# Column roll by 100 on one core: head loads of 1280 B between 256 B boundaries, in place of 1024 B that begin 112 B past one

## The chip, the cores and the metric

The kernel runs on one core of one Trainium2 chip. The metric is device time in microseconds (us). Timed alone, the kernel before took 817.23 us, the median of three runs (817.18 to 818.21). Every other time here is from one profiled execution of it.

## The reference

The kernel shifts each row of an 8192 x 8192 float32 matrix by 100 columns, cyclically:

```python
def reference(x, shift):            # x: 8192 x 8192 float32, shift = 100
    return np.roll(x, shift, axis=1)
```

So out[r, 100:] is x[r, :8092], and out[r, :100] is x[r, 8092:]. Nothing is calculated: 268 MB are read and 268 MB are written.

## The kernel before, in words

The kernel cuts each output row at column a = 256. With s = 100 (the shift), the head of a row is its first 256 columns, of which the first s come from the end of the same input row and the other g = a - s = 156 from its beginning. The bulk is the rest, columns 256 to 8191.

**The bulk** (lines 36 to 43) never enters the core's own memory. Two hardware queues, SP's and ACT's, issue 264 copies each from DRAM to DRAM. Most of them have 16 rows of 7936 floats (31,744 B a row, 496 KB a copy); in the last four blocks each is cut into two halves of 248 KB. All of it goes out from one line, L43, in the order of the loop, j = 0 and 2 from SP and j = 1 and 3 from ACT.

**The heads** (lines 60 to 80) go through SBUF, the core's own memory, and all their DMAs are issued by POOL (GpSimd). A stage k takes 512 rows: 128 partitions with Q = 4 neighbouring rows each; there are 16 stages. The last 100 columns of row r and the first 156 of row r + 1 are neighbours in DRAM, so one run of 256 floats (1024 B) that straddles the row boundary brings the wrapped part of one row and the beginning of the next. A stage does this:

- L72 loads t, [128, 3, 256]: for each partition the three straddling runs between its four rows. 128 x 3 = 384 runs of 1024 B, 384 KB.
- L73 loads the last 100 columns of the fourth row straight into h, 400 B a partition.
- L74 (DVE) copies the wrapped parts of rows 0 to 2 from t to h, 300 floats a partition.
- L76 loads the first 156 columns of row 0 straight into h, 624 B a partition.
- L77 (DVE) copies the beginnings of rows 1 to 3 from t to h, 468 floats a partition.

After the 16 stages of loads, L80 issues 16 stores of h (512 KB each, rows of 1024 B) into the output. Both pools have 16 buffers, so no tile waits for another to come free. POOL's instructions stand in the program's order: all loads, then all stores. From the ninth POOL DMA on, each waits for an earlier one's semaphore, of which there are eight.

The line that the change is about is the address of the straddling run (L70 and L71):

```python
lead = bass.AP(tensor=x.tensor, offset=(k * P * Q + 1) * n_cols - s,
               ap=[[Q * n_cols, P], [n_cols, Q - 1], [1, a]])
```

A row of x has 32,768 B, a multiple of 256. A run begins 400 B ahead of a row's beginning, which is 112 B past a 256 B boundary, and ends 624 B behind it, which is 144 B short of one.

Of the kernel before, what the change touches and what calls it, by code (L numbers as in the profile page):

```python
# [1 line left out]

# [4 lines left out]


@with_exitstack
def kernel(  # L10
    ctx: ExitStack,
    tc: tile.TileContext,
    x: bass.AP,
    shift: int,
    out: bass.AP,
):
    nc = tc.nc
    n_rows, n_cols = x.shape
    s = shift % n_cols
    a = -(-s // 128) * 128  # L20
    if 0 < a <= 384 and a + 128 <= n_cols:
        a += 128
    g = a - s
    P = nc.NUM_PARTITIONS
    engines = [nc.sync, nc.scalar]
    n_chunks = 16
    rows = n_rows // n_chunks

    xm = x.rearrange("(c e j) w -> c j e w", e=16, j=4)
    om = out.rearrange("(c e j) w -> c j e w", e=16, j=4)
    if a < n_cols:
        blocks = n_rows // 64
        mid = (a + n_cols) // 256 * 128
        for c in range(blocks):
            parts = ((a, mid), (mid, n_cols)) if c >= blocks - 4 and a < mid else ((a, n_cols),)  # L40
            for j in range(4):
                for lo, hi in parts:
                    engines[j % 2].dma_start(out=om[c, j, :, lo:hi], in_=xm[c, j, :, lo - s:hi - s])  # L43
    if a == 0:
        return


    if a > 512:
        for i in range(n_chunks):
            r = slice(i * rows, (i + 1) * rows)  # L50
            nc.gpsimd.dma_start(out=out[r, :s], in_=x[r, n_cols - s:])
            if g > 0:
                nc.gpsimd.dma_start(out=out[r, s:a], in_=x[r, :g])
        return

    Q = 4  # L60
    n_st = n_rows // (P * Q)
    reads = ctx.enter_context(tc.tile_pool(name="reads", bufs=n_st))
    heads = ctx.enter_context(tc.tile_pool(name="heads", bufs=n_st))
    xt = x.rearrange("(k p q) c -> k p q c", q=Q, p=P)
    ot = out.rearrange("(k p q) c -> k p q c", q=Q, p=P)
    tiles = []
    for k in range(n_st):
        t = reads.tile([P, Q - 1, a], x.dtype)
        h = heads.tile([P, Q, a], x.dtype)
        lead = bass.AP(tensor=x.tensor, offset=(k * P * Q + 1) * n_cols - s,  # L70
                       ap=[[Q * n_cols, P], [n_cols, Q - 1], [1, a]])  # L71
        nc.gpsimd.dma_start(out=t[:], in_=lead, single_packet=True)  # L72
        nc.gpsimd.dma_start(out=h[:, Q - 1, :s], in_=xt[k, :, Q - 1, n_cols - s:], single_packet=True)  # L73
        nc.vector.tensor_copy(h[:, :Q - 1, :s], t[:, :, :s])  # L74
        if g > 0:
            nc.gpsimd.dma_start(out=h[:, 0, s:], in_=xt[k, :, 0, :g], single_packet=True)  # L76
            nc.vector.tensor_copy(h[:, 1:, s:], t[:, :, s:])  # L77
        tiles.append(h)
    for k, h in enumerate(tiles):
        nc.gpsimd.dma_start(out=ot[k, :, :, :a], in_=h[:], single_packet=True)  # L80


# [1 line left out]
_INS = ['x', 'shift']  # L84
_OUTS = [((8192, 8192), 'float32')]

_NUMBERS = {'shift': 100}


# [26 lines left out]
```

## Time and profile before

| what | value |
|---|---|
| median of three timed runs | 817.23 us (817.18 to 818.21) |
| profiled execution, span from first to last instruction | 813.9 us |
| what the timed median has beyond that span | 3.3 us |
| DVE busy | 12.0 us, 1% of the span, 32 copies |
| POOL busy | 41.1 us, 5% of the span, 68 instructions |
| bulk copies: moved by queues q1 and q10 | 260.08 MB |
| heads: moved by queue q0 | 16.78 MB (8.39 loaded, 8.39 stored) |
| straddling load t<-in_x_dram | 16 of 384 KB, 48.9 us from issue to landing (median) |
| head store out_dram<-h | 16 of 512 KB, 102.9 us from issue to landing (median) |
| bulk copy of 496 KB | 12.5 us from issue to landing (median) |

The span is the time of the profiled execution; its page gives no time beyond the span, so what lies around it is taken from the timed median. In the profile's page, q1 and q10 are the two hardware queues (bulk), q0 is POOL's software queue (heads). The share of a DMA queue is the time that its packets took, over the 16 DMA engines' time. A packet that waits for its data counts as taking time, so a share near 100% does not say that an engine moves bytes at its own limit. A DRAM-to-DRAM byte is counted once in MB and GB/s, but is read from DRAM once and written to it once; a byte of a head load or store touches DRAM once only.

### The profile page before, as it was taken

How to read it: one execution, taken by the hardware profiler on the slowest of the kernel's cores; microseconds unless marked ns; L12 is line 12 of the kernel's file. 1: busy time of each engine (PE TensorE's matmuls, PEld its weight loads, DVE VectorE, ACT ScalarE, POOL GpSimd, SP SyncE). 2: the span in 40 equal slices, each digit the busy share in tenths (PEclk: the TensorE clock that was granted, in tenths of full speed). 3: DMA queues.
4: the chain of work that ended last, by engine and by line, in shares of the span. 5: the costliest groups of instructions: out<-in, count | busy, mean ns of one | idle time of the engine just before them, and what ended most of it. 6: DMA issues, size and time to landing. Idle time of an engine off the chain costs nothing. (4 is left out here: it accounts for less than half of the span.)

```text
span 813.9 us, 689 instructions
## 1 busy us (share of the span) xinstructions
DVE 12.0 (1%) x32; POOL 41.1 (5%) x68
## 2 busy tenths in 40 slices
DVE  0000000000000000000000000000000000000000
POOL 2000011111000100000000000000000000000000
DMA  9999999999999999999999999999999999999998
GB/s 314 346 340 344 353 346 350 344 351 344 346 355 346 345 362 354 353 357 354 355 355 349 342 335 331 335 332 325 335 328 332 334 337 334 332 337 332 334 314 293
DMA packets 22277, 276.90 MB, mean 340 GB/s; under 512 B 9472, under 2 KB 9728, under 8 KB 13824
## 3 DMA queue, kind: packets, MB, share of 16 engines
q1 hardware_dynamic: 8448, 130.04, 45.9%
q10 hardware_dynamic: 8448, 130.04, 44.3%
q0 software_dynamic: 5376, 16.78, 8.9%
q14 instruction: 5, 0.04, 0.0%
HBM read 268.44 MB, written 268.44 MB: 660 GB/s over the span
## 5 line engine op out<-in xcount | busy, mean ns | idle before, releaser
L80 POOL DMA_DIRECT2D out_dram<-h x16 | 11.4, 713 | 139.5 <-DMA out_dram<-h 92.5
L76 POOL DMA_DIRECT2D h<-in_x_dram x16 | 8.6, 540 | 158.4 <-DMA t<-in_x_dram 158.4
L72 POOL DMA_DIRECT2D t<-in_x_dram x16 | 12.2, 760 | 32.1 <-DMA h<-in_x_dram 31.3
L73 POOL DMA_DIRECT2D h<-in_x_dram x16 | 8.9, 558 | 32.7 <-DMA h<-in_x_dram 32.7
L74 DVE COPY h<-t 128x300 f32<-128x300 f32 x16 | 5.9, 367 | 268.4 <-DMA t<-in_x_dram 268.4
L77 DVE COPY h<-t 128x468 f32<-128x468 f32 x16 | 7.5, 468 | 0.0
L97 POOL MEMSET const-float32-0.0<- 128x1 f32 x1 | 0.1, 98 | 0.2 <-issue 0.2
L97 POOL MEMSET const-bfloat16-1.0<- 128x1 bf16 x1 | 0.1, 101 | 0.0
L97 POOL MEMSET const-float32-1.0<- 128x1 f32 x1 | 0.1, 98 | 0.0
L97 POOL MEMSET const-uint8-127<- 128x1 uint8 x1 | 0.1, 98 | 0.0
## 6 DMA issues: line engine op xcount, KB each, us to landing
out_dram<-in_x_dram ACTq DMA_DIRECT2D x248, 496.0 KB, 12.5
out_dram<-in_x_dram SPq DMA_DIRECT2D x248, 496.0 KB, 12.5
out_dram<-h POOLq DMA_DIRECT2D x16, 512.0 KB, 102.9
t<-in_x_dram POOLq DMA_DIRECT2D x16, 384.0 KB, 48.9
out_dram<-in_x_dram SPq DMA_DIRECT2D x16, 248.0 KB, 5.9
out_dram<-in_x_dram ACTq DMA_DIRECT2D x16, 248.0 KB, 5.9
h<-in_x_dram POOLq DMA_DIRECT2D x16, 78.0 KB, 41.9
h<-in_x_dram POOLq DMA_DIRECT2D x16, 50.0 KB, 47.2
```

Of the source, the lines that this page charges most:

```text
L72: nc.gpsimd.dma_start(out=t[:], in_=lead, single_packet=True)
L73: nc.gpsimd.dma_start(out=h[:, Q - 1, :s], in_=xt[k, :, Q - 1, n_cols - s:], single_packet=True)
L74: nc.vector.tensor_copy(h[:, :Q - 1, :s], t[:, :, :s])
L76: nc.gpsimd.dma_start(out=h[:, 0, s:], in_=xt[k, :, 0, :g], single_packet=True)
L77: nc.vector.tensor_copy(h[:, 1:, s:], t[:, :, s:])
L80: nc.gpsimd.dma_start(out=ot[k, :, :, :a], in_=h[:], single_packet=True)
L97: nc = _bacc.Bacc("TRN2", target_bir_lowering=False, num_devices=1)
```

## The change

The straddling run is widened at both ends to the next multiple of 64 floats (256 B): lo = 128 floats ahead of the row's beginning (100 are used) and hi = 192 floats behind it (156 are used). A run has 320 floats, 1280 B, and begins and ends on a 256 B boundary. The tile t grows to [128, 3, 320], 480 KB a stage. The two DVE copies take the same 300 and 468 floats out of the middle of the runs. All other loads, the stores and the bulk are as they were, and so is the order of the instructions on every engine.

```diff
     Q = 4
+    lo, hi = -(-s // 64) * 64, -(-g // 64) * 64
...
-        t = reads.tile([P, Q - 1, a], x.dtype)
+        t = reads.tile([P, Q - 1, lo + hi], x.dtype)
         h = heads.tile([P, Q, a], x.dtype)
-        lead = bass.AP(tensor=x.tensor, offset=(k * P * Q + 1) * n_cols - s,
-                       ap=[[Q * n_cols, P], [n_cols, Q - 1], [1, a]])
+        lead = bass.AP(tensor=x.tensor, offset=(k * P * Q + 1) * n_cols - lo,
+                       ap=[[Q * n_cols, P], [n_cols, Q - 1], [1, lo + hi]])
         nc.gpsimd.dma_start(out=t[:], in_=lead, single_packet=True)
         nc.gpsimd.dma_start(out=h[:, Q - 1, :s], in_=xt[k, :, Q - 1, n_cols - s:], single_packet=True)
-        nc.vector.tensor_copy(h[:, :Q - 1, :s], t[:, :, :s])
+        nc.vector.tensor_copy(h[:, :Q - 1, :s], t[:, :, lo - s:lo])
         if g > 0:
             nc.gpsimd.dma_start(out=h[:, 0, s:], in_=xt[k, :, 0, :g], single_packet=True)
-            nc.vector.tensor_copy(h[:, 1:, s:], t[:, :, s:])
+            nc.vector.tensor_copy(h[:, 1:, s:], t[:, :, lo:lo + g])
```

## The prediction

> **What bounds the kernel now.** I read the engines' row first, then the DMA rows of the page, then who SP waits for, then the DMA queues stage by stage.
>
> ```profile
> DVE 12.0 (1%) x32; POOL 41.1 (5%) x68
> ...
> DMA  9999999999999999999999999999999999999998
> ...
> q1 hardware_dynamic: 8448, 130.04, 45.9%
> q10 hardware_dynamic: 8448, 130.04, 44.3%
> q0 software_dynamic: 5376, 16.78, 8.9%
> ...
> HBM read 268.44 MB, written 268.44 MB: 660 GB/s over the span
> ```
>
> No engine computes for long; the DMA engines are never free. The chain of waits is of no use here: it follows POOL and stops at 403 us, while bulk copies are issued until 807 us. SP's own waits name what ends last:
>
> ```profile
> SPq L43 <- DMA out_dram<-in_x_dram: 667.0, 260, 4.5
> ```
>
> For 667 of 814 us SP waits for earlier bulk copies to land. So the kernel ends when the bulk ends, and the heads cost only what they take away from it. What do the two share? Three windows tell: 20 to 280 us (head loads beside the bulk), 290 to 410 us (head stores beside it), 520 to 780 us (bulk alone). Columns: packets, MB, share of the 16 DMA engines.
>
> ```profile
> q1 hardware_dynamic: 2572, 40.83, 41.9%
> q10 hardware_dynamic: 2568, 40.70, 39.5%
> q0 software_dynamic: 3136, 8.69, 18.4%
> ```
>
> ```profile
> q1 hardware_dynamic: 1183, 18.79, 46.5%
> q10 hardware_dynamic: 1182, 18.76, 42.3%
> q0 software_dynamic: 1406, 5.11, 12.2%
> ```
>
> ```profile
> q10 hardware_dynamic: 2726, 43.24, 49.9%
> q1 hardware_dynamic: 2728, 43.30, 49.6%
> ```
>
> Count a bulk byte twice (read and written in DRAM) and a head byte once. Loads: (2 x 81.53 + 8.69) MB / 260 us = 660.6 GB/s. Stores: (2 x 37.55 + 5.11) / 120 = 668.4. Bulk alone: 2 x 86.54 / 260 = 665.7. Counted simply, the rates are 347, 356 and 333 GB/s and differ by 7%; as DRAM traffic they agree within 1.2%. **The bound is DRAM traffic, about 660 to 668 GB/s in every stage**, whoever asks for it. All traffic over the rate of bulk alone, (2 x 260.08 + 16.78) MB / 665.7 GB/s, gives 806.6 us of the 813.9; 2.0 us more is the lower rate beside the loads (5.1 GB/s x 260 us = 1.33 MB), and the other 5.3 us lie in the start, the tail and the edges of my windows.
>
> **The change part by part.**
>
> *More bytes read.* 16 loads x 384 runs x 256 B = 1.573 MB more from DRAM (t goes from 6.29 to 7.86 MB). They are asked for in the load stage, so they cost 1.573 MB / 660.6 GB/s = **2.4 us**, by which the bulk, and with it the end, moves back. This is the one term on the path.
>
> Whether 256 B more that is asked for is 256 B more that DRAM delivers, the trace of before does not show. Ends: at the low end the shortfall of the load stage (1.33 MB, 2.0 us) is all waste at the ends of the misaligned runs, fetched already and thrown away, and the change costs 2.4 - 2.0 = +0.4 us; zero is possible within the scatter of that shortfall. At the high end DMA engine time is what is short: q0 took 18.4% of 260 us = 47.8 us for 8.69 MB beside the loads, 5.51 us per MB, so 1.573 MB would take 8.7 us (at the stores' price, 12.2% of 120 us for 5.11 MB = 2.86 us per MB, 4.5 us). I take 2.4 us, since the three stages agree in DRAM traffic and in no other count, and keep the ends.
>
> The load stage being the one that is below the others speaks for some waste there. The Trainium skill (DMA: Bandwidth & Descriptors, "How a descriptor splits into AXI transactions") says that a read which starts off a 256 B boundary begins its first transaction at the boundary below, and that the bytes ahead of its start still cost 32 B beats. By it I estimate 8 + 24 + 4 = 36 beats for 1024 B from 112 past a boundary, and 40 beats for 1280 aligned ones: 128 B more per run, 0.79 MB, 1.2 us in place of 2.4. So even by that rule the aligned run is the dearer one. Nothing in the sum rests on this.
>
> *More bytes written to SBUF.* The same 1.573 MB, off DRAM. Covered as long as DRAM is short; if engine time is, their price is in the 4.5 to 8.7 us above.
>
> *POOL's issues.* 16 loads of t at 0.75 us each, 384 runs each before and after: 0. Behind each stand POOL's later loads, and L76 waits 158.4 us in all for landings of t:
>
> ```profile
> POOL h L76 <- DMA t<-in_x_dram: 158.4, 14, 14.5
> POOL out_dram L80 <- DMA out_dram<-h: 92.5, 7, 16.1
> ```
>
> With 19% more to load (8.39 to 9.96 MB) at the same share (8.69 MB in 260 us, 33 GB/s) the load stage would last some 47 us longer, and the stores would shift with it. Cover: the last packets of q0 lie between 500 and 520 us (five of them), and there is none after. A shift of 47 us leaves some 250 us of bulk behind them. Cost 0; were that cover gone, it would be the full 47 us. No SP or ACT instruction waits for POOL or DVE.
>
> *DVE's copies.* The same 300 and 468 floats (367 and 468 ns), read from other places of a wider tile. 12.0 us in all, in 814. Even doubled, 12 us spread over the load stage move only the stores. Cost 0 under the same cover.
>
> *SBUF room and buffers.* t takes 61,440 B a partition instead of 49,152; 16 buffers for 16 stages, so no wait is added.
>
> **Sum:** +2.4 us. Span 813.9 + 2.4 = 816.3 us. The median of the runs stands 3.3 us above the span, for start and end outside it, which the change does not touch: **819.6 us**, 0.3% slower. About 0.2%, 1.6 us, is what a measurement of this kernel can tell from no change, so this is close to that edge.
>
> **The rivals.**
>
> *The extra bytes are fetched already (same).* From 400 B ahead of a row to 624 B behind it, or from 512 to 768, a run touches the same five blocks of 256 B. If DRAM hands out whole blocks, nothing is added. For it: the load stage's 660.6 against 665.7 and 668.4; thrown-away bytes of 256 per run would be 1.57 MB, and 1.33 are missing. Against it: 0.8% is of the size by which the other two stages differ (0.4%) and a little more; small runs may cost it by themselves. Time: 817.2 to 818.4, most likely 817.6 us (+0.4). The page's 1.2 us lies inside.
>
> *Engine time is the bound (slower).* Price 4.5 to 8.7 us: 821.7 to 825.9 us. For it: the queues' shares add to 99%. Against it: bulk moves 81.53 MB in 81.4% of 260 us, 385 GB/s of its own time, beside loads, and 86.54 in 99.5%, 334, alone; it is faster in the time it has while q0 holds the engines, so their time is not what is fixed.
>
> *A misaligned start slows the load packets, and slow packets hold the bulk up (faster).* Place: t's packets in the load stage. q0 takes 5.51 us per MB there and 2.86 beside the stores, whose runs of 1024 B are aligned in DRAM. If alignment brings t to the stores' price, t falls from 6.29 x 5.51 = 34.7 to 7.86 x 2.86 = 22.5 us: 12.2 us faster, 805.0 us, if engine time ends last. It begins to count as faster when the load stage passes (171.75 + 1.57) MB / 258.4 us = 671 GB/s of DRAM traffic. Against it: no stage is above 668.4, and loads wait for DRAM where stores read SBUF, which explains the dearer packets without alignment. At 668.4 the stage would be 0.7 us shorter, not a visible gain.
>
> *That it does not do what it says:* the built program holds loads of 128 x 3 x 320 in the old order, so only a cut of the 1280 B runs into pieces would be possible; I keep no chance for it.
>
> **How the numbers follow.** Forecast (bytes count, +2.4) 0.47; fetched already 0.36; engine time 0.07; misaligned packets 0.10. Slower by over 0.2%: 0.47 + 0.07 = 0.54. Within: 0.36. Faster: 0.10. Range 815.6 to 821.7: it holds the forecast and the first rival with 1.6 us of scatter below no change, reaches to the near end of the engine-time case, and leaves out the faster case and the dear end. The forecast's own range is 818.9 to 820.5.
>
> **What would show it.** In the profile after, t is 16 x 480 KB and q0 moves 18.35 MB. If the forecast is right, the load stage has again about 661 GB/s of DRAM traffic, counted by bytes asked for, and bulk alone 666. If "fetched already" is right, the load stage rises to about 666 and the span stays near 814. If engine time is the bound, traffic in the load stage falls below 655. If alignment helps, q0's price in the load stage falls from 5.5 towards 2.9 us per MB, and traffic passes 671. In every case q0 should be silent by some 560 us; head stores that reach towards 800 us would make the whole argument wrong, and so would packets of q0 far above 5376 + 1536.

## The result and the profile after

The changed kernel takes 819.82 us (median of 11 runs, 818.05 to 820.78), the kernel before beside it 817.23 (11 runs, 816.36 to 819.32). The ratio is 1.0023, 95% interval 1.0013 to 1.0032: the change costs 1.9 us (1.1 to 2.6). The two medians by themselves lie 2.6 us apart, at the upper edge of this interval. The profiled execution has a span of 816.6 us, 2.7 more than before's.

The page of the kernel after: engines, slices, DMA queues, DRAM.

```profile
DVE 12.0 (1%) x32; POOL 41.3 (5%) x68
...
DMA  9999999999999999999999999999999999999998
...
q1 hardware_dynamic: 8448, 130.04, 45.9%
q10 hardware_dynamic: 8448, 130.04, 44.5%
q0 software_dynamic: 5376, 18.35, 8.5%
...
HBM read 270.01 MB, written 268.44 MB: 659 GB/s over the span
```

The bulk is the same 260.08 MB. q0 has the same 5376 packets and 1.57 MB more, all of it read. Its packets took a smaller share than before, 8.5% against 8.9%, which is 69.4 us of the 16 engines' time against 72.4: if busy DMA engines were what a kernel pays for, this one would be faster.

SP's waits, after:

```profile
SPq L43 <- DMA out_dram<-in_x_dram: 670.3, 258, 5.0
```

SP still waits for bulk copies, 3.3 us more in all. Now the three windows of the prediction (packets, MB, share): 20 to 280 us, head loads beside the bulk.

```profile
q1 hardware_dynamic: 2551, 40.48, 42.2%
q10 hardware_dynamic: 2546, 40.35, 39.9%
q0 software_dynamic: 3052, 9.86, 17.2%
```

290 to 410 us, head stores beside the bulk:

```profile
q1 hardware_dynamic: 1184, 18.83, 46.5%
q10 hardware_dynamic: 1189, 18.99, 43.4%
q0 software_dynamic: 1313, 4.77, 10.8%
```

520 to 780 us, bulk alone:

```profile
q10 hardware_dynamic: 2727, 43.30, 49.8%
q1 hardware_dynamic: 2726, 43.27, 49.5%
...
q0 software_dynamic: 2, 0.00, 0.0%
```

With a bulk byte counted twice and a head byte once, the DRAM traffic is (2 x 80.83 + 9.86) / 260 = 659.7 GB/s beside the loads (before 660.6), (2 x 37.82 + 4.77) / 120 = 670.1 beside the stores (668.4), and 2 x 86.57 / 260 = 665.9 alone (665.7). The rates stand and the heads take more of the traffic: in the first window they moved 1.17 MB more and the bulk 0.70 MB less. This window also holds the first head stores, issued from 255 us on before and from 264 us after; over 20 to 240 us, with loads alone beside the bulk, the traffic is 660.6 GB/s before and 657.6 after. The whole account shows from 0 to 520 us, where all but two of the heads' packets lie. First before, then after:

```profile
q1 hardware_dynamic: 5142, 81.88, 44.2%
q10 hardware_dynamic: 5133, 81.59, 41.7%
q0 software_dynamic: 5376, 16.78, 13.9%
```

```profile
q1 hardware_dynamic: 5118, 81.50, 44.2%
q10 hardware_dynamic: 5107, 81.15, 42.0%
q0 software_dynamic: 5374, 18.35, 13.3%
```

By 520 us the heads have moved 1.57 MB more and the bulk 0.82 MB less, which is 1.64 MB of traffic; the traffic is 661.0 GB/s before and 660.9 after. At the 333 GB/s of the bulk alone, 0.82 MB take 2.5 us, of the 2.7 by which the span grew. That is the whole change in these two executions: what the heads read in excess, the bulk gets later.

### The profile page after: what moved, and what is told of

The parts are those of the page before. It is cut to its first block, busy times and chain, and to the rows that moved or that the text cites. A ratio compares the mean times of both kernels' runs of the same rounds, so it can differ in the third digit from the quotient of the medians.

```text
span 816.6 us, 689 instructions
## 1 busy us (share of the span) xinstructions
DVE 12.0 (1%) x32; POOL 41.3 (5%) x68
## 3 DMA queue, kind: packets, MB, share of 16 engines
q0 software_dynamic: 5376, 18.35, 8.5%
## 4 chain that ended last, share of the span: by engine, by line
DMA 33%; another core or an unknown queue 16%; POOL 1%; issue 1%; POOLq 0%; PEldq 0%
DMA h<-in_x_dram 16%; DMA t<-in_x_dram 11%; DMA out_dram<-h 6%; POOL out_dram L81 1%; POOL h L74 0%; POOL h L77 0%; POOL t L73 0%; POOLq L112 0%; POOLq L81 0%; PEldq L112 0%
## 5 line engine op out<-in xcount | busy, mean ns | idle before, releaser
L74 POOL DMA_DIRECT2D h<-in_x_dram x16 | 8.9, 559 | 33.4 <-DMA h<-in_x_dram 33.4
## 6 DMA issues: line engine op xcount, KB each, us to landing
t<-in_x_dram POOLq DMA_DIRECT2D x16, 480.0 KB, 51.9
```

## The experiments

Four theories, all named in the expectations below: A, the bytes asked for count, at the rate of the DRAM traffic; B, DRAM hands out whole blocks of 256 B, so that the misaligned run already cost 1280; C, DMA engine time is short; D, a misaligned start slows the loads and through them the bulk. Each kernel was timed beside the kernel before on the same chip. Microseconds below are (ratio - 1) times the median of before beside it: 828.89 on the chip of the first four, 817.92 for the three after, 817.12 and 815.87 for the last five.

### Length and alignment of the straddling runs

The changed kernel again.

> The changed kernel once more, as the base of the two runs beside it. Theory A (the DRAM bytes asked for count, at about 661 GB/s beside the loads): +2.4 us over before, ratio 1.003. Theory B (DRAM hands out whole 256 B blocks; 1024 B from 112 past a boundary and 1280 aligned bytes touch the same five): 0 to +0.4 us, ratio 1.000. Theory C (DMA engine time is short): +4.5 to +8.7 us.

Measured: ratio 1.0021 (1.0003 to 1.0039), +1.7 us (0.2 to 3.2). The same result on a chip whose bulk runs at a lower rate (652.4 GB/s of traffic from 520 to 780 us, against 665.9); the interval is too wide to tell A from B by itself.

The same 1280 B, 112 B past a boundary:

```diff
-    lo, hi = -(-s // 64) * 64, -(-g // 64) * 64
+    lo, hi = s, 320 - s
```

> Runs of 1280 B as in the changed kernel, but beginning 112 B past a 256 B boundary as before (from 400 B ahead of the row to 880 B behind it). The output stays the same. Theory A: as the changed kernel, +2.4 us over before; 0 between the two. Theory B: six blocks where the changed kernel touches five, so 1.57 MB more than it, 2.4 us slower than the changed kernel. Theory D (a misaligned start slows the load packets and these hold the bulk up): slower than the changed kernel, and q0's price in the load stage about a quarter or more above the changed kernel's 4.5 us per MB.

Measured: 1.0039 (1.0022 to 1.0057), +3.2 us (1.8 to 4.7), which is 1.5 us above the changed kernel with an uncertainty of about 2. That fits A's 0 and B's 2.4 alike and decides nothing between them. It does speak against D's second sign, dearer loads. Its window of 20 to 280 us:

```profile
q0 software_dynamic: 4060, 13.53, 20.8%
```

20.8% of 260 us is 54.1 us for 13.53 MB, 4.0 us per MB, against 18.6% for 10.27 MB, 4.7, in the aligned kernel's profile beside it. Stores had begun in this window, which makes the mean cheaper, so the figure is no price of misalignment; but the loads were not held up. The rows of DVE's first copy, which follows each landing of t, give the end of the load stage by the start of their last copy. First the aligned kernel beside it, then the misaligned one:

```profile
L75 DVE COPY h<-t x16: 367/367/368, 21.4 to 295.3; 128x300 f32<-128x300 f32 x16
```

```profile
L75 DVE COPY h<-t x16: 366/368/369, 20.9 to 224.6; 128x300 f32<-128x300 f32 x16
```

In these two executions the misaligned loads were done 71 us earlier, the opposite of D, and the kernel was not faster for it. Why they were earlier is not shown.

The same 1024 B as before, aligned:

```diff
-    lo, hi = -(-s // 64) * 64, -(-g // 64) * 64
+    lo, hi = 128, 128
...
-            nc.vector.tensor_copy(h[:, 1:, s:], t[:, :, lo:lo + g])
+            nc.vector.tensor_copy(h[:, 1:, s:], t[:, :, lo + hi - g:])
```

> Runs of 1024 B as before, but beginning and ending on 256 B boundaries (512 B to both sides of the row's beginning). This kernel leaves out 28 columns of each head's run that are not loaded; it copies others in their place, so that all instructions keep their sizes. Theory A: the bytes of before, 0 us against before, ratio 1.000. Theory B: four blocks in place of five, 1.57 MB less, -2.4 us, ratio 0.997. Theory D: up to 12 us faster, and at least some of it.

Measured: 0.9994 (0.9981 to 1.0008), -0.5 us (-1.6 to +0.7). B's 0.997 lies outside, and so does any large gain after D. **Alignment alone, at the same length, is worth 0.5 us here, and 1.6 us at the most; nothing at all is within the interval.**

Five times the extra bytes, aligned:

```diff
-    lo, hi = -(-s // 64) * 64, -(-g // 64) * 64
+    lo, hi = 256, 320
```

> Runs of 2304 B between 256 B boundaries (1024 B ahead of the row, 1280 behind): five times the extra bytes of the change, 1280 B more per run than before, 7.86 MB in all. The output stays the same. Theory A: 7.86 MB / 660.6 GB/s = +11.9 us over before, ratio 1.0146. Theory B: nine blocks in place of five, 6.29 MB more, +9.5 us. Theory C: 7.86 MB at 2.86 to 5.51 us per MB, +22 to +43 us. If the extra bytes were hidden: 0.

Measured: 1.0164 (1.0141 to 1.0187), +13.6 us (11.7 to 15.5). A's +11.9 is at the lower edge of the interval, B's +9.5 is outside, and C's 22 is far off. The extra bytes cost 13.6 / 7.86 = 1.73 us per MB; A's price is 1.51. **The length is what the change pays for**, and the price is A's or somewhat above it.

### Engine time or DRAM bytes

Three kernels put 8.39 MB behind the head stores of the kernel before, for the most part beside bulk that ran alone there (the first of them go out at 369 to 413 us, while the last stores are under way). They differ in where the data comes from.

```diff
+    extra = ctx.enter_context(tc.tile_pool(name="extra", bufs=n_st))
...
+    for i in range(1 * n_st):
+        k = i % n_st
+        e = extra.tile([P, Q, a], x.dtype)
+        nc.gpsimd.dma_start(out=e[:], in_=tiles[k][:], single_packet=True)
```

> The kernel before, with 16 DMAs from SBUF to SBUF (h into a tile that nobody reads, 512 KB each, 8.39 MB in all) behind the head stores in POOL's queue, so beside bulk that used to run alone. It adds DMA engine time and SBUF traffic and no DRAM byte. Theory A: 0 us, ratio 1.000, as long as the copies end before the bulk does. Theory C: at the stores' price of 2.86 us per MB, +24 us, ratio 1.029.

Measured: 1.0002 (0.9991 to 1.0013), +0.2 us. C's 24 us are excluded. The window of 520 to 700 us of this kernel shows why:

```profile
q1 hardware_dynamic: 1896, 30.03, 46.7%
q10 hardware_dynamic: 1887, 29.91, 45.8%
q0 software_dynamic: 1485, 5.38, 7.3%
```

q0 takes 7.3% of the engines' time, the bulk's share shrinks from 99.5% to 92.5%, and the bulk moves at 2 x 59.94 / 180 = 666.0 GB/s of DRAM traffic, as fast as alone. **DMA engines that were busy 99% of the time had room**: part of a bulk packet's time is waiting, and not for an engine. Since the traffic is what stays the same, I read it as waiting for DRAM; whether the memory itself or the way to it is the limit, no run here separates. The copies also write 8.39 MB into SBUF, so the prediction's second term, more bytes written there, cost nothing visible.

The same with loads from DRAM, `in_=xt[k, :, :, 2048:2048 + a]`:

> The kernel before, with 16 loads from DRAM to SBUF in the same place as the SBUF copies of its twin (512 rows of 1024 B each, columns 2048 to 2303, aligned to 256 B; 8.39 MB that nobody reads). Theory A: 8.39 MB / 665.7 GB/s = +12.6 us, ratio 1.0154. Theory C: 24 us or more. If a read in the shade of the bulk is hidden: 0.

Measured: 1.0234 (1.0211 to 1.0256), +19.1 us (17.3 to 20.9), half as much again as A's 12.6. And with `in_=xt[k, :, :, 2048 + 28:2048 + 28 + a]`:

> As x_al1024, but the rows of 1024 B begin 112 B past a 256 B boundary (28 columns further on). Theory A: as x_al1024, +12.6 us over before. Theory B: five blocks in place of four for each of 8192 runs, 2.1 MB more, 3.2 us slower than x_al1024, +15.8 us over before. Theory D: slower than x_al1024 and dearer in q0's time per MB.

Measured: 1.0195 (1.0171 to 1.0218), +15.9 us (14.0 to 17.8). The misaligned twin is the faster by some 3 us, give or take 2.7; B and D both had it slower. That B's 15.8 us for it is met is luck, since B had 12.6 for the aligned one. Neither meets A's 12.6, so A lacks something. In the aligned kernel the DRAM traffic is 662 GB/s while the loads run (440 to 540 us), about as forecast; most of the loss lies where they end. Its window of 560 to 600 us (first what was moved in each of 40 slices, then the queues):

```profile
GB/s 408 415 363 192 500 414 263 387 465 284 324 238 406 342 149 206 188 268 333 348 314 512 417 362 353 349 258 417 159 444 290 290 317 317 254 381 163 0 508 127
...
q1 hardware_dynamic: 360, 5.71, 41.8%
q10 hardware_dynamic: 350, 5.49, 33.9%
q0 software_dynamic: 423, 1.52, 14.8%
```

A slice here is one microsecond. There are holes, down to 0 and 127 GB/s near the end, and the traffic is (2 x 11.20 + 1.52) / 40 = 598 GB/s: 2.7 MB short of 665.7, 4.1 us, most of the 6.5 us that A missed. The queues' shares add up to 90.5% here, so the engines stand idle in part of it, while SP waits up to 8.0 us for a bulk copy to land (5.3 us from 440 to 540 us). Here, then, it is not traffic that is short. What makes the holes stays open.

### Short runs, without the heads

To settle alignment, four kernels keep the bulk and replace the heads by 24 loads of 512 KB that nobody reads, 12.58 MB; they leave out the first 256 columns of the output. They differ in `off` (2048 or 512 columns, 28 more where misaligned) and in the runs: 4 of 256 floats per partition, or 16 of 64.

```diff
+    for i in range(24):
+        k = i % n_st
+        e = extra.tile([P, 16, 64], x.dtype)
+        runs = bass.AP(tensor=x.tensor, offset=k * P * Q * n_cols + off,
+                       ap=[[Q * n_cols, P], [2048, 16], [1, 64]])
+        nc.gpsimd.dma_start(out=e[:], in_=runs, single_packet=True)
```

> Leaves out the heads (the first 256 columns of the output). The bulk as it was, and beside it from the start 24 loads from DRAM to SBUF that nobody reads, each 512 runs of 1024 B on 256 B boundaries: 12.58 MB. Theory A (bytes asked for count): the bulk alone, about 790 us by 520.16 MB / 665.7 GB/s and 8.6 us around it, and 18.9 us more, 809 us, ratio to before 0.990.

> As b1024_al (the heads are left out), but each run begins 112 B past a 256 B boundary. Theory A: no difference from b1024_al. Theory B (whole 256 B blocks): five blocks in place of four, 3.1 MB more, +4.7 us. By the beats that I counted after the Trainium skill (DMA: Bandwidth & Descriptors, How a descriptor splits into AXI transactions), 36 in place of 32, it would be +2.4 us, an estimate. Theory D: slower, with q0 dearer per MB.

> Leaves out the heads too. As b1024_al, but the same 12.58 MB come in runs of 256 B on 256 B boundaries, 2048 runs a load. Theory A: 18.9 us above the bulk alone, ratio to before 0.990, as b1024_al.

> As b256_al (the heads are left out), but each run of 256 B begins 112 B past a boundary. Theory A: no difference from b256_al. Theory B: two blocks in place of one, 12.58 MB more, +18.9 us. By the beats, 12 in place of 8, +9.4 us, an estimate. This run tells the three apart best, since the waste is as large as the run itself.

And the bulk alone, with no loads at all:

> Leaves out the heads and all loads beside the bulk: the 528 bulk copies alone. It is the base for the loads beside the bulk. Theory A: 520.16 MB of DRAM traffic at 665.7 GB/s and 8.6 us around it, 790 us, ratio to before 0.967. Then 12.58 MB of aligned 1024 B runs, at ratio 0.997, cost 30 thousandths of 817 us, some 24 us or 1.95 us per MB, and not the 1.5 us per MB of the sum. If theory A's price holds for those loads (18.9 us), this kernel takes 795 us, ratio 0.973.

| kernel | ratio to before | interval |
|---|---|---|
| bulk alone | 0.9662 | 0.9646 to 0.9677 |
| 1024 B aligned | 0.9968 | 0.9952 to 0.9985 |
| 1024 B misaligned | 0.9964 | 0.9946 to 0.9981 |
| 256 B aligned | 0.9992 | 0.9977 to 1.0006 |
| 256 B misaligned | 1.0067 | 1.0047 to 1.0087 |

At 1024 B alignment makes -0.3 us, give or take 2 (the intervals of the two added in squares): A's 0 fits, B's +4.7 doesn't, and the +2.4 of the counted beats lies just outside. At 256 B it makes +6.1 us, give or take 2: neither A's 0 nor B's 18.9. So misaligned runs of 256 B do cost more, but less than a block: if the 6.1 us are all wasted DRAM traffic, they are 6.1 us x 665.7 GB/s = 4.06 MB over 49,152 runs, some 83 B a run (55 to 110). The estimate by the counted beats (DMA: Bandwidth & Descriptors of the Trainium skill, "How a descriptor splits into AXI transactions") had the right sign; with 128 B a run, 9.4 us, it is above the interval. The pages of the two kernels differ in the same way; first 256 B aligned, then misaligned:

```profile
q0 software_dynamic: 3456, 12.58, 7.3%
```

```profile
q0 software_dynamic: 3456, 12.58, 9.5%
```

Same packets, same bytes, and 78 us of the 16 engines' time instead of 60. For the 1024 B pair the two shares are 7.2% aligned and 6.7% misaligned. The row of DRAM bytes tells nothing here: it says that 272.63 MB were read in all four, which is what was asked for. So the waste in traffic is a reading, and engine time is a rival to it: from 20 to 180 us the shares of the three queues add up to 99 to 100% in these four kernels and q0 takes 26 to 29%, where x_sbuf, which found room, asked for 7.3%. No run separates the two.

The bulk alone came out as the traffic rule has it (0.967 expected). The 1024 B loads cost 0.9968 - 0.9662, 25.0 us, for 12.58 MB: 1.99 us per MB, not A's 1.50 (the two ratios are from two chips). In the kernel before, 16.78 MB of heads cost 0.0338 x 815.87 = 27.6 us, 1.64 per MB, half of them stores.

## Why the prediction was right

**The bound.** DRAM traffic: shown by the copies from SBUF to SBUF (no cost at 7.3% of the engines' time), by the bulk alone, and by three stages that kept their traffic within 0.3% when the heads grew. The rate does not hold for every load: in the four kernels of short runs the traffic is 643 to 656 GB/s from 20 to 180 us.

**The 2.4 us for more bytes.** The interval is 1.1 to 2.6 us, so sign and size hold, and the two sides of the term have been moved one at a time: length without misalignment (wide2304) costs 11.7 to 15.5 us for five times the bytes, and alignment without length (al1024) gives between -1.6 and +0.7. As the rule behind the number, "bytes asked for at the DRAM rate" is only roughly true, on two sides. A misaligned run costs something, some 83 B by the 256 B pair if it is all DRAM traffic; if that holds for runs of 1024 B, which was not measured with such accuracy, the change saves 0.5 MB and its net is (256 - 83) x 6144 = 1.06 MB, 1.6 us. On the other side loads from DRAM beside the bulk cost 1.7 to 2.3 us per MB in wide2304, b1024_al and x_al1024 and not 1.5; where the extra time was looked for, in x_al1024, it lay mostly in holes at the end of the loads. The two errors have opposite signs, and the runs can't tell 1.6 from 2.4 us in this change, nor either from the 1.2 us that the prediction estimated by the counted beats. That 2.4 us is the best of the three is not shown.

**The 3.3 us around the span** was added to the forecast span of 816.3: the span was 816.6, and that execution took 818.36 us, so 1.8 us lay around it, as in every run on record (1.7 to 1.8). So the 3.3 us were not all start and end: some 1.5 of them say that the profiled execution of before was quicker than its median. The profiled execution after is 1.5 us under its median too, and that the two agree is luck.

**POOL's issues at no cost.** Right in effect, wrong in size. I expected the load stage to last 47 us longer at the same share. The rows of DVE's first copy, which follows each landing of t, give its end; before, then after:

```profile
L74 DVE COPY h<-t x16: 366/367/368, 20.7 to 279.7; 128x300 f32<-128x300 f32 x16
```

```profile
L75 DVE COPY h<-t x16: 367/368/368, 20.8 to 290.9; 128x300 f32<-128x300 f32 x16
```

The last copy moved from 279.7 to 290.9 us, 11 us. The head loads do not have a fixed rate: from 20 to 280 us q0 moved 33.4 GB/s before (8.69 MB) and 37.9 after (9.86). I had called this window head loads, though five stores were issued in it; from 20 to 240 us, with loads alone, it is 32.5 and 37.6. With eight DMAs of POOL's queue in flight, a longer load took little longer to land: 51.9 us at the median instead of 48.9, for a quarter more bytes. The cover was there as stated: after 520 us q0 has two packets left. The runs bear it out: al1024, after_again and mis1280, on one chip, have their last copy at 318.9, 295.3 and 224.6 us, and the one whose loads end last is the fastest (it also reads the least).

**The rivals.** "Fetched already" (0.36) had the right element, that a misaligned run costs more than its bytes, but that shows at 256 B only and is far less than a block there; the interval of the change excludes its likeliest +0.4 us. "Engine time" fell with x_sbuf, and with the change itself: the packets of q0 took 3.0 us less of the engines' time and the kernel became slower. "Misaligned packets" showed one of its two signs: q0's price beside the loads fell from 5.51 to 17.2% x 260 us / 9.86 MB = 4.54 us per MB. But alignment is not what brought it down: al1024, aligned, has 15.5% x 260 / 7.78 = 5.18, and of the two with 1280 B the misaligned one is the cheaper (4.46 against 4.95 from 20 to 190 us, before any store). The traffic, which I had named as the point that decides, stayed at 659.7 GB/s and not above 671. Cheaper packets were worth nothing, since the engines' time was not what was short.

**Open:** whether DRAM itself or the way to it is the limit; whether the loads that cost more than 1.5 us per MB, and the misaligned ones of 256 B, pay in traffic or in engine time; why misaligned loads of 1280 B were done earlier than aligned ones; what makes the holes where loads beside the bulk end; why x_mis1024 was faster than its aligned twin when the pair without heads shows no difference; and what part of the 83 B a 1024 B run wastes.

## What to carry to other kernels

Before a transfer is padded to a boundary, find the resource that the stage is short of, by a count that comes out alike in all stages (here each byte once for every touch of DRAM), and price the padding in it: 25% more bytes per run cost more than the alignment returned. In these runs alignment showed only where runs were as short as the block, 256 B. A DMA engine that the profile shows as 99% busy may be waiting for memory, and a kernel that adds DMA work without DRAM bytes tells.

## What the runs showed that was not expected

- Copies within SBUF, 8.39 MB beside a saturated bulk, cost 0.2 us (-0.7 to 1.1), while loads of as many bytes from DRAM at the same point of the program cost 15.9 and 19.1 us.
- Such loads cost 1.7 to 2.3 us per MB, where the rate of the DRAM traffic gives 1.5; in x_al1024 4.1 us of it was a stretch of 40 us at 598 GB/s where the loads ran out.
- Misalignment by 112 B cost 6.1 us for 49,152 runs of 256 B and nothing measurable for 12,288 runs of 1024 B.
- The load stage ended at 224.6 us with misaligned runs of 1280 B and at 295.3 us with aligned ones, and the kernel's time did not follow.
